# Mixer of a hybrid encoder: inverse norm roots by one GpSimd power, a bias negated on ScalarE, S5 steps earlier in the order

## The chip, the core and the metric

The kernel runs on one core of one Trainium2 chip. The metric is the device time of one execution in microseconds (us); the median of 3 runs of the kernel before is 2024.78 us (2024.78 to 2025.44). The core's engines each take their instructions from a queue of their own, strictly in order: TensorE (PE, matmuls and transposes), VectorE (DVE), ScalarE (ACT), GpSimd (POOL), and SyncE (SP, which issues the DMAs). They meet through semaphores only.

## What is computed

A trunk of two layers on x of 512 positions by 1024 features, all in float32. Each layer is a feed-forward block, a mixer with four head groups, and a second feed-forward block:

```python
for layer in range(DEPTH):                     # DEPTH = 2
    x = x + 0.5 * swiglu(rms_norm(x, ffn1_norm[layer]), ffn1_w_in[layer], ffn1_w_out[layer])
    x = x + hybrid_mixer(rms_norm(x, mix_norm[layer]), w_in[layer], ...)
    x = x + 0.5 * swiglu(rms_norm(x, ffn2_norm[layer]), ffn2_w_in[layer], ffn2_w_out[layer])

def hybrid_mixer(h, w_in, ...):
    aq, ak, av, bu, cq, ck, cv, dq, dk, dv = jnp.split(h @ w_in, splits, axis=-1)
    o_a, lse_a = banded_attention(rms_norm(heads(aq), ...), rms_norm(heads(ak), ...), heads(av), ...)
    y_b = s5_bidirectional(bu, lam_re, lam_im, ...)          # a complex diagonal recurrence, both ways
    y_b = g * jax.nn.sigmoid(g @ w_glu)                      # g = gelu(y_b)
    o_c = dilated_attention(rms_norm(heads(cq), ...), rms_norm(heads(ck), ...), heads(cv), ...)
    o_d = neighborhood_attention(rms_norm(heads(dq), ...), rms_norm(heads(dk), ...), heads(dv), rel_bias)
    return concatenate([o_a, y_b, o_c, o_d]) @ w_out
```

The queries and keys of groups A, C and D (aq, ak, cq, ck, dq, dk) are each scaled by the inverse root of their mean square: six norms in a mixer, twelve in the kernel. Five of the six have four heads (16 numbers to a partition), ak has two (8 numbers). Group D adds a learned relative bias and a mask to its scores.

## The kernel before, in words

**Products.** A float32 product is made of three matmuls, mm3 (L106 to L109): each operand is split into a high part, rounded to a type that the matmul takes, and the low remainder. weights() (L116 to L134) loads a block of weights (wr), rounds it on ScalarE (wh, L125) and subtracts on VectorE (wl, L126); in the mixer the subtraction is given to GpSimd instead (pooled=True).

**The mixer's pieces.** project() runs a projection of 512 positions as steps of matmuls into ppr. qk() (L549 to L606) takes a q or k projection: ScalarE copies it (L565) and squares it, VectorE sums the squares (L570), adds epsilon (L573, the tile ss), takes the inverse root (rn) and multiplies (four instructions at L579). flip() then transposes the result on TensorE (ptp, L589) and splits it in high (o, by ScalarE) and low (L603, by VectorE). s5() runs the recurrence: matmuls er and ei (per, pei), four VectorE products with the rotation (L810 to L813, out of PSUM), two GpSimd sums (zr, zi, L814 and L815), four scans on VectorE (sr, si, L823 and L825), the rotation back (zr, zi at L832 to L837, partly on GpSimd as rot), and matmuls pyp (L847 to L849). Attention heads: scores psc, the sum with the bias and its maximum p, mn (L680), exponentials on ScalarE, a scaling of p on GpSimd (L694), transposes (L713), copies pT (L715, L716), products pot (L718, L719), and the head's result m, split by L736 and L737 into mt. The merges mA to mD multiply mt by w_out (pop).

**The inverse root.** rsqrt() (L136 to L145) is eleven VectorE instructions: a shift and a subtraction on the bits as integers for a first guess (L140, L141), then three rounds of three (L143 to L145).

**What sets the order.** ORDER (L34 to L39) is a string of 116 tokens, written by hand: dq, dk, dv, cq and so on are a projection's steps (the fifth of a q or k is its flip), s5 the recurrence's steps, Ds and Dt (Cs, Ct, As, At) the two halves of a head, mB a merge step. The program is written out in this order; on each engine a scheduler places the instructions, and from then on each queue is fixed. Nothing is reordered at run time. Tile names carry a number in what follows (rn669 is one tile); tiles of before and of after have different numbers.

Of the kernel before, what the change touches and what calls it, by code (L numbers as in the profile page):

```python
# [32 lines left out]
BIG = 1e30  # L33
HOOK = 300  # L34
ORDER = """
dq dq dq dk dk dq dq dk s5 dk dv cq dk s5 Ds dv dv ck cq ck Ds cq dv Ds dv Ds Ds s5 cq s5 Dt ck s5 Dt s5 Dt ck
cq s5 Ds cv Dt aq cv s5 aq Ds Dt Dt Ds ck Cs cv Dt s5 cv aq ak aq Cs s5 ak Dt Cs aq Cs Ct ak mD ak Cs Ct Cs Cs
Ct ak Cs Ct s5 mD Ct mD As Ct As Ct Ct As mD As As At As As mB At As At At At mC mC mB mB mC At At mC At mC mC
mC mB mC mA mA  # L39
"""  # L40
T2 = 15
# [29 lines left out]
def hybrid_encoder(ctx: ExitStack, tc: tile.TileContext, t: dict):  # L71
# [61 lines left out]

        return at  # L134

    def rsqrt(y, v, shape):  # L136
        w = sml([P, 16], "rq")
        w = w[:, :shape[0]] if len(shape) == 1 else w.rearrange("p (a b) -> p a b", a=shape[0])[:, :, :shape[1]]
        yi = y.bitcast(I32)
        ts(yi, v.bitcast(I32), 1, None, op0=ALU.logical_shift_right)  # L140
        ts(yi, yi, -1.0, float(0x5F3759DF), op0=ALU.mult, op1=ALU.add)  # L141
        for _ in range(3):
            tt(w, y, y, op=ALU.mult)  # L143
            stt(w, w, -0.5, v, op0=ALU.mult, op1=ALU.mult)
            stt(y, w, 1.5, y, op0=ALU.add, op1=ALU.mult)  # L145

    ident = pool.tile([P, P], F32, name="ident")
    make_identity(nc, ident)
    ones2 = pool.tile([P, 2], F32, name="ones2")
    nc.vector.memset(ones2, 1.0)  # L150
    mhalf = pool.tile([P, 4], F32, name="mhalf")
    nc.vector.memset(mhalf, -0.5)
    ebase = pool.tile([P, G], F32, name="ebase")
    nc.vector.memset(ebase, E32)
# [11 lines left out]

    qkg = pool.tile([P, DEPTH, 6], F32, name="qkg")
    sink = pool.tile([P, DEPTH, 4], F32, name="sink")
    dmask = pool.tile([P, 7, 16], F32, name="dmask")
    for tl, nme in ((qkg, "qkg"), (sink, "sink"), (dmask, "dmask")):  # L170
        nc.gpsimd.dma_start(tl, t[nme])
    for i in (0, 2, 4):
        ts(qkg[:, :, i], qkg[:, :, i], -1.0, None, op0=ALU.mult)
# [314 lines left out]
    def mixer(l, T, next_norm):  # L488
# [63 lines left out]
        def qk(blk0, nh, perm, gi, res, extra=None):  # L552
# [4 lines left out]
            def norm():  # L557
                pts = st["pts"]
                if extra is not None:
                    extra(pts)  # L560
                ss = sml([P, 4, 4], "ss")
                for j in range(2):
                    q = t2(name="q")
                    qv = q.rearrange("p (b w) -> p b w", b=2)[:, :, :w]
                    nc.scalar.copy(qv, pts[j].rearrange("p (b w) -> p b w", b=2)[:, :, :w])  # L565
                    raw.append(qv)
                    sq = t2(name="sq")
                    sv = sq.rearrange("p (b w) -> p b w", b=2)[:, :, :w]
                    act(sv, qv, AF.Square)
                    nc.vector.tensor_reduce(ss[:, 2 * j:2 * j + 2, :nh], sv.rearrange("p b (h d) -> p b h d", d=64),  # L570
                                            axis=AX.X, op=ALU.add)
                sn = ss[:, :, :nh]
                tt(sn, sn, bc(ec, 2, nh), op=ALU.add)  # L573
                rn = sml([P, 4, 4], "rn")
                rsqrt(rn[:, :, :nh], sn, [4, nh])
                for j in range(2):
                    for b in range(2):
                        a = raw[j][:, b].rearrange("p (h d) -> p h d", d=64)
                        tt(a, a, bc(rn[:, 2 * j + b, :nh], 2, 64), op=ALU.mult)  # L579
# [81 lines left out]
        def attention(res, qk, vs, band, biases, perm, is_a):  # L661
# [35 lines left out]
            def second(i, part):  # L697
# [36 lines left out]
                if i % 2 == 1:  # L734
                    mt = k4([P, 2, S], F32R, name="mt")
                    nc.scalar.copy(mt[:, 0], m)  # L736
                    gtt(mt[:, 1], m, f32(mt[:, 0]), op=ALU.subtract)  # L737
                    res[i // 2].append(mt)

            return first, second  # L740
# [38 lines left out]

        def d_bias(i):  # L780
            b = bias_tile(t["rbx"][l, i], 896, True)
            for c0, m0, nk in ((0, 0, 2), (256, 2, 3), (640, 5, 2)):
                bv = b[:, c0:c0 + nk * P].rearrange("p (k u w) -> p k u w", u=8, w=16)
                tt(bv, bc(dmask[:, m0:m0 + nk], 2, 8), bv, op=ALU.subtract)
            return lambda q: b[:, 0:256] if q == 0 else (b[:, 640:896] if q == 3 else b[:, 256:640])

        def c_bias(i):
# [162 lines left out]
def _tables():  # L950
# [8 lines left out]
    mult = (dist <= 64) * 1 + ((dist % 4 == 0) & (dist <= 256)) * 1 + (dist % 16 == 0) * 1  # L959
    for i in range(4):  # L960
        ctab[i] = np.where(mult > 0, slopes[4 + i] * dist - np.log(np.maximum(mult, 1)), BIG)
    dmask = np.zeros((P, 7, 16), np.float32)
    ri = np.zeros((P, 896), np.int64)
    ci = np.zeros((P, 896), np.int64)
    r, c = np.arange(P) // 16, np.arange(P) % 16
    for qb, k0, k1, col, m0 in ((0, 0, 2, 0, 0), (1, 0, 3, 256, 2), (3, 2, 4, 640, 5)):
        qc = 16 * qb + c
        ws = np.clip(qc - 8, 0, 48)
        for kb in range(k0, k1):
            for u in range(8):  # L970
                for w in range(16):
                    kc = 16 * kb + w
                    j = col + (kb - k0) * P + u * 16 + w
                    dmask[:, m0 + kb - k0, w] = np.where((kc >= ws) & (kc < ws + 16), 0.0, BIG)
                    ri[:, j] = u - r + 7
                    ci[:, j] = np.clip(kc - qc + 15, 0, 30)
    return atab, ctab, dmask, ri, ci


def _layout(i):  # L980
# [56 lines left out]
        for c in range(16):  # L1037
            sd[:, 64 * (g % 2) + c, 3 * (g // 6) + g % 6 // 2, c] = dsk[:, g, c]
    a["s5d"] = sd
    a["atab"], a["ctab"], a["dmask"], ri, ci = _tables()  # L1040
    a["rbx"] = ac(np.asarray(i["na_rel_bias"])[:, :, ri, ci])
    return a


# [14 lines left out]
```

## Time and profile before

| | before |
|---|---|
| median of 3 runs | 2024.78 us |
| the profiled execution, its own time | 2025.69 us |
| its span in the trace | 2023.9 us |
| TensorE busy | 1969.1 us, 97% of the span |
| VectorE, ScalarE, GpSimd busy | 1240.6, 804.4, 368.4 us (61%, 40%, 18%) |

The profiled execution stands 0.9 us above the median; 1.8 us of it lie outside the span. The two mixers take up about 404 to 665 us and 1408 to 1669 us of the span and show the same pattern of waits; the times quoted from here on are those of the first. A line's number is that of the kernel before. "Idle before" is how long an engine stood still ahead of an instruction, and the name behind the arrow is whose semaphore came last. PEclk is the granted clock of TensorE as a share of its full speed: 1.00 is 2.4 GHz, 0.50 is 1.2 GHz.

### The profile page before, as it was taken

To read this page: it belongs to the slowest core of one execution; us is meant where nothing else is said; L and a number is where in the kernel's file an instruction comes from. 1 tells how busy PE (TensorE), PEld (TensorE's weight loads), DVE (VectorE), ACT (ScalarE), POOL (GpSimd) and SP (SyncE) were. 2 spreads that over 40 slices of the span, in tenths; PEclk is the share of its full clock that TensorE was granted. 3 is DMA by queue.
4 is the path that set the end of the run, shared out by engine and by line. 5 is a ranking of instruction groups with operands and counts; after the bars stand their busy time and mean duration, and the time that the engine had idled before them with its cause. 6 is when DMAs were issued, how large, how long until landed. Compare 5 with 4: busy or idle time off the path is not lost.

```text
span 2023.9 us, 26161 instructions
## 1 busy us (share of the span) xinstructions
PE 1969.1 (97%) x9768; PEld 1648.9 (81%) x9768; DVE 1240.6 (61%) x2327; ACT 804.4 (40%) x1523; POOL 368.4 (18%) x349
## 2 busy tenths in 40 slices
PE   8999999998999999999999999999989989999999
PEld 6788878897977788888888888888978778888887
DVE  6865547657887545444577655465687875444454
ACT  4333323444676323233442333334547653232332
POOL 4010100254445000000120101002544540000000
PEclk9999999998999999999999999999989999999999
DMA  5232343331312332323233332423313122333233
GB/s 176 82 104 88 104 83 106 97 114 51 97 55 72 97 101 91 97 89 109 84 116 88 102 93 93 102 88 103 119 39 99 50 66 94 99 96 103 81 107 104
DMA packets 74447, 189.24 MB, mean 93 GB/s; under 512 B 16960, under 2 KB 22848, under 8 KB 74320
## 3 DMA queue, kind: packets, MB, share of 16 engines
q1 hardware_dynamic: 74224, 187.51, 30.7%
q8 instruction: 76, 1.25, 0.3%
q14 instruction: 51, 0.42, 0.1%
q0 software_dynamic: 96, 0.07, 0.0%
HBM read 182.86 MB, written 4.69 MB: 93 GB/s over the span
## 4 chain that ended last, share of the span: by engine, by line
PE 83%; DVE 10%; ACT 4%; issue 2%; POOL 1%; DMA 0%; SPq 0%; DVEq 0%; ACTq 0%; POOLq 0%
PE pop L109 9%; PE pop L108 9%; PE pop L107 9%; PE pup L107 7%; PE pgp L107 7%; PE pgp L108 7%; PE pgp L109 7%; PE pup L109 7%; PE pup L108 7%; PE ppr L107 1%; PE ppr L108 1%; PE ppr L109 1%; DVE wl L126 1%; PE pfp L448 1%; DVE hl L186 1%
## 5 line engine op out<-in xcount | busy, mean ns | idle before, releaser
L125 ACT CAST wh<-wr 128x512 fp32r<-128x512 f32 (+2 forms) x718 | 405.9, 570 | 962.8 <-PE pgp L109 314.0
L126 DVE TENSOR_TENSOR wl<-wr,wh 128x512 fp32r<-128x512 f32 (+2 forms) x618 | 409.4, 665 | 380.0 <-ACT wh L125 378.3
L107 PE MATMUL pgp<-hh,wl 128*128 128x512 f32 x704 | 275.5, 391 | 7.6 <-DVE wl L126 7.6
L107 PE MATMUL pup<-hh,wl 128*128 128x512 f32 x704 | 276.3, 392 | 3.2 <-DVE wl L126 3.2
L107 PE MATMUL pop<-a,wl 128*128 128x512 f32 x704 | 277.0, 395 | 1.4 <-DVE wl L126 1.4
L108 PE MATMUL pgp<-hl,wh 128*128 128x512 f32 x704 | 275.5, 391 | 2.4 <-DVE hl L186 2.4
L109 PE MATMUL pop<-a,wh 128*128 128x512 f32 x704 | 276.3, 392 | 0.0
L108 PE MATMUL pop<-a,wh 128*128 128x512 f32 x704 | 274.5, 390 | 0.6 <-DVE a L257 0.6
L108 PE MATMUL pup<-hl,wh 128*128 128x512 f32 x704 | 275.0, 391 | 0.0
L109 PE MATMUL pup<-hh,wh 128*128 128x512 f32 x704 | 275.0, 391 | 0.0
L109 PE MATMUL pgp<-hh,wh 128*128 128x512 f32 x704 | 274.7, 390 | 0.0
L196 POOL TENSOR_TENSOR t<-t,sq 128x512 f32<-128x512 f32 x42 | 60.0, 1430 | 664.9 <-ACT sq L195 663.6
L107 PEld LDWEIGHTS pgp<-hh,wl 128*128 128x128 f32 x704 | 132.6, 188 | 35.7 <-DVE wl L126 8.0
L126 POOL TENSOR_TENSOR wl<-wr,wh 128x512 fp32r<-128x512 f32 (+1 forms) x100 | 131.2, 1317 | 161.7 <-ACT wh L125 125.4
L107 PEld LDWEIGHTS pup<-hh,wl 128*128 128x128 f32 x704 | 132.5, 188 | 33.6 <-DVE wl L126 5.6
L108 PEld LDWEIGHTS pgp<-hl,wh 128*128 128x128 f32 x704 | 132.6, 188 | 32.9 <-DVE hl L186 5.5
L109 PEld LDWEIGHTS pop<-a,wh 128*128 128x128 f32 x704 | 132.2, 188 | 30.6
L108 PEld LDWEIGHTS pop<-a,wh 128*128 128x128 f32 x704 | 132.2, 188 | 30.2 <-DVE a L257 1.0
L107 PEld LDWEIGHTS pop<-a,wl 128*128 128x128 f32 x704 | 132.3, 188 | 28.9 <-DVE wl L126 2.1
L109 PEld LDWEIGHTS pup<-hh,wh 128*128 128x128 f32 x704 | 132.4, 188 | 27.6
L109 PEld LDWEIGHTS pgp<-hh,wh 128*128 128x128 f32 x704 | 132.4, 188 | 27.6
L108 PEld LDWEIGHTS pup<-hl,wh 128*128 128x128 f32 x704 | 132.5, 188 | 27.4
(263 smaller groups left out, 3071.3 us busy)
## 6 DMA issues: line engine op xcount, KB each, us to landing
wr<-in_f_w SPq DMA_DIRECT2D x176, 512.0 KB, 3.4
wr<-in_f_w SPq DMA_DIRECT2D x64, 384.0 KB, 3.1
wr<-in_f_w SPq DMA_DIRECT2D x64, 320.0 KB, 2.9
wr<-in_wm SPq DMA_DIRECT2D x36, 512.0 KB, 3.5
bias<-in_ctab SPq DMA_DIRECT2D x8, 448.0 KB, 3.4
bias<-in_rbx SPq DMA_DIRECT2D x8, 448.0 KB, 3.8
wr<-in_woC SPq DMA_DIRECT2D x8, 384.0 KB, 3.1
x<-in_xt SPq DMA_DIRECT2D x8, 256.0 KB, 6.4
```

Source lines behind the costliest of these rows:

```text
L107: nc.tensor.matmul(out, ll, rh, start=start, stop=False)
L108: nc.tensor.matmul(out, lh, rl, start=False, stop=False)
L109: nc.tensor.matmul(out, lh, rh, start=False, stop=stop)
L125: nc.scalar.copy(hi[:, :w], r)
L126: (nc.gpsimd if pooled else nc.vector).tensor_tensor(lo[:, :w], r, f32(hi[:, :w]), op=ALU.subtract)
L186: stt(hl, x[c], gcol, f32(hh), op0=ALU.mult, op1=ALU.subtract)
L196: gtt(acc, acc, sq, op=ALU.add)
L448: nc.tensor.matmul(pt[r0:r0 + 64, c0 + 16:c0 + 144], bm[q][:, g].rearrange("p a c -> p (a c)"), v[q][:, g].rearrange("p j c -> p (j c)"), ...
```

## The change

Four edits, all in the mixer:

- rsqrt() goes. The norm's root is one GpSimd power, rn = ss to the power of -0.5 (gtt at L567 of after), over 128x16 for four heads and 128x8 for ak's two; the tile of exponents mhalf is widened to 16.
- The low half of mt (L737) moves from GpSimd to VectorE.
- D's bias: before, VectorE subtracts it from a mask in three instructions for a head (L784); now the mask is put into the bias on the host and ScalarE negates it by one copy with a scale of -1 over 128x896.
- ORDER: S5's steps come sooner. The first stands after the third dq instead of after the third dk.

```diff
-dq dq dq dk dk dq dq dk s5 dk dv cq dk s5 Ds dv dv ck cq ck Ds cq dv Ds dv Ds Ds s5 cq s5 Dt ck s5 Dt s5 Dt ck
-cq s5 Ds cv Dt aq cv s5 aq Ds Dt Dt Ds ck Cs cv Dt s5 cv aq ak aq Cs s5 ak Dt Cs aq Cs Ct ak mD ak Cs Ct Cs Cs
-Ct ak Cs Ct s5 mD Ct mD As Ct As Ct Ct As mD As As At As As mB At As At At At mC mC mB mB mC At At mC At mC mC
+dq dq dq s5 dq s5 dk dk dk dq dk s5 dv s5 dk dv cq s5 Ds dv s5 dv ck cq ck Ds s5 cq dv Ds s5 Ds Ds cq Dt ck Dt
+Dt ck cq Ds cv Dt aq cv aq Ds s5 Dt Dt Ds ck Cs cv Dt cv aq ak aq s5 Cs ak Dt Cs aq Cs s5 Ct ak mD ak Cs Ct Cs
+Cs Ct ak Cs Ct mD Ct mD As Ct As Ct Ct As mD As As At As As mB At As At At At mC mC mB mB mC At At mC At mC mC
...
-                rsqrt(rn[:, :, :nh], sn, [4, nh])
+                if nh == 4:
+                    sn, rv, half = (a.rearrange("p b h -> p (b h)") for a in (ss, rn, mhalf.rearrange("p (b h) -> p b h", b=4)))
+                else:
+                    rv, half = rn[:, :, :nh], mhalf.rearrange("p (b h) -> p b h", b=4)[:, :, :nh]
+                gtt(rv, sn, half, op=ALU.pow)
...
-                    gtt(mt[:, 1], m, f32(mt[:, 0]), op=ALU.subtract)
+                    tt(mt[:, 1], m, f32(mt[:, 0]), op=ALU.subtract)
...
-            for c0, m0, nk in ((0, 0, 2), (256, 2, 3), (640, 5, 2)):
-                bv = b[:, c0:c0 + nk * P].rearrange("p (k u w) -> p k u w", u=8, w=16)
-                tt(bv, bc(dmask[:, m0:m0 + nk], 2, 8), bv, op=ALU.subtract)
+            act(b[:, :896], b[:, :896], AF.Copy, scale=-1.0)
```

On the engines this makes VectorE's queue 2130 instructions long instead of 2274, GpSimd's 343 instead of 344, ScalarE's 1435 instead of 1429; outside the two mixers no queue changes its order.

**VectorE, cq's norm, before.** The place is the end of cq's norm in the first mixer (ss773 to rn778), among S5's rotation back (zi682) and the copies of D's first head (pT):

```order
L140 TENSOR_SCALAR rn778_4158<-ss773_4146 128x16
L141 TENSOR_SCALAR rn778_4158<-rn778_4158 128x16
L143 TENSOR_TENSOR rq779_4159<-rn778_4158 128x16
L144 SCALAR_TENSOR_TENSOR rq779_4159<-rq779_4159,ss773_4146 128x16
L145 SCALAR_TENSOR_TENSOR rn778_4158<-rq779_4159,rn778_4158 128x16
...
L837 TENSOR_TENSOR zi682_3640<-zi682_3640,rot791_4233 128x512
L145 SCALAR_TENSOR_TENSOR rn778_4158<-rq779_4159,rn778_4158 128x16
L716 TENSOR_TENSOR pT795_4253<-ptp794_4249,pT795_4253 128x384
L579 TENSOR_TENSOR q774_4147<-q774_4147,rn778_4158 128x256 x2
```

S5's zi stands behind ten of the norm's eleven instructions; the norm's products with q follow.

**VectorE, dk's norm, after.** S5's scans now come during D's projections. This is the queue from dq's products (q667, the second half) to dk's (q691, q693, with rn695):

```order
L571 TENSOR_TENSOR q667_3528<-q667_3528,rn669_3534 128x256 x2
...
L561 TENSOR_TENSOR ss690_3704<-ss690_3704,ec636_3348 128x16
L813 SCALAR_TENSOR_TENSOR si697_3723<-k480_2623,zi659_3471 64x1023
L815 SCALAR_TENSOR_TENSOR si697_3723<-k480_2623,zi659_3471 64x1023
...
L813 SCALAR_TENSOR_TENSOR sr696_3722<-k480_2623,zr658_3470 64x1023
L815 SCALAR_TENSOR_TENSOR sr696_3722<-k480_2623,zr658_3470 64x1023
L825 TENSOR_TENSOR zi659_3471<-si697_3723,k478_2621 128x512 x2
...
L632 TENSOR_TENSOR vb711_3803<-a710_3801,R635_3346 128x8x4x16
L571 TENSOR_TENSOR q691_3705<-q691_3705,rn695_3716 128x256 x2
L571 TENSOR_TENSOR q693_3710<-q693_3710,rn695_3716 128x256 x2
```

Between dk's sum of squares (ss690) and its products now stand four scans, two products of S5 and three low halves of dq (left out here, o at L595). Before, dk's products followed its eleven small instructions directly, with no scan between.

**GpSimd, the same stretch, before**, in the mixer's D projections:

```order
L126 TENSOR_TENSOR wl680_3612<-wr676_3605,wh679_3611 128x512
L126 TENSOR_TENSOR wl696_3723<-wr694_3720,wh695_3722 128x512
L815 TENSOR_TENSOR zi682_3640<-zi682_3640,rot686_3660 128x512
L814 TENSOR_TENSOR zr681_3639<-zr681_3639,rot685_3659 128x512
L126 TENSOR_TENSOR wl698_3727<-wr694_3720,wh697_3726 128x512
L126 TENSOR_TENSOR wl702_3746<-wr700_3743,wh701_3745 128x512
```

**and after**, with the two powers of dq (rn669) and dk (rn695):

```order
L804 TENSOR_TENSOR zr658_3470<-zr658_3470,rot662_3490 128x512
L567 TENSOR_TENSOR rn669_3534<-ss664_3522,mhalf_70 128x16
L805 TENSOR_TENSOR zi659_3471<-zi659_3471,rot673_3559 128x512
L804 TENSOR_TENSOR zr658_3470<-zr658_3470,rot672_3558 128x512
L126 TENSOR_TENSOR wl683_3629<-wr681_3626,wh682_3628 128x512
L126 TENSOR_TENSOR wl685_3633<-wr681_3626,wh684_3632 128x512
...
L567 TENSOR_TENSOR rn695_3716<-ss690_3704,mhalf_70 128x16
L126 TENSOR_TENSOR wl714_3808<-wr712_3805,wh713_3807 128x512
L823 TENSOR_TENSOR rot719_3841<-si697_3723,k479_2622 128x512
L126 TENSOR_TENSOR wl716_3812<-wr712_3805,wh715_3811 128x512
L826 TENSOR_TENSOR rot720_3842<-sr696_3722,k479_2622 128x512
L126 TENSOR_TENSOR wl730_3869<-wr728_3866,wh729_3868 128x512
```

S5's sums come ahead of the weights of dv and cq, a power stands between them, and four weights and two rotations follow the second power.

**TensorE, S5's result, before and after.** Before, one matmul of pyp818 that reads zi682 stands among cq's projection and D's heads, and the rest right behind it:

```order
L109 MATMUL ppr830_4422<-wh788_4204,hh580_3121 128x256
L718 MATMUL pot780_4181<-pT795_4253,v757_4063 128x384
L849 MATMUL pyp818_4362<-zi682_3640,s279_1564 128x64
L847 MATMUL pyp818_4362<-u2640_3359,tm414_2319 128x64
L848 MATMUL pyp818_4362<-zr681_3639,s278_1563 128x64
```

After, dk's transposes (ptp704, ptp707) and, 100 rows behind them, S5's pyp751, all 24 matmuls in one piece:

```order
L109 MATMUL ppr718_3816<-wh701_3736,hh580_3119 128x256
L581 MATMUL ptp704_3759<-ident_63,q691_3705 128x2x4x16
L581 MATMUL ptp707_3774<-ident_63,q691_3705 128x2x4x16
L107 MATMUL ppt733_3876<-hh589_3153,wl716_3812 128x512
...
L109 MATMUL ppr743_3923<-wh731_3872,hh580_3119 128x256
L837 MATMUL pyp751_4016<-u2640_3357,tm414_2317 128x64
L838 MATMUL pyp751_4016<-zr658_3470,s278_1561 128x64
L839 MATMUL pyp751_4016<-zi659_3471,s279_1562 128x64
```

S5's result is asked for earlier in the mixer, right behind D's v and the first scores, and dk's transposes come 92 rows behind dq's.

## Rows read from the trace of the kernel before

**Rows 1.** The page's part 1: each engine's busy us, share, instructions.
```profile
PE 1969.1 (97%) x9768; PEld 1648.9 (81%) x9768; DVE 1240.6 (61%) x2327; ACT 804.4 (40%) x1523; POOL 368.4 (18%) x349
```
**Rows 2.** Window: length, busy us (count) of PE, PEld, DVE, ACT, POOL, PEclk, DMA.
```profile
475.00:500.00 25.00, 17.51 (x108) 16.58 (x108) 20.99 (x39) 6.80 (x16) 13.76 (x12) 0.77 0.14 43
```
**Rows 3.** TensorE's waits over the whole span: us in total, times, longest.
```profile
PE pyp L849 <- DVE zi L837: 11.3, 2, 5.7
PE pot L719 <- DVE pT L716: 5.8, 8, 1.2
...
PE pop L107 <- ACT mt L885: 3.2, 2, 1.6
...
PE pop L108 <- POOL mt L737: 2.3, 4, 0.9
```
**Rows 4.** Timeline of TensorE, the longest wait: start, us, instruction, [idle before <-releaser].
```profile
491.90 0.69 PE L849 MATMUL pyp<-zi,s 128*128 128x64 f32 x2 [5.67 <-DVE zi L837]
```
**Rows 5.** Windows of 4 us at 488 and at 588 (PEclk third from right).
```profile
488.00:492.00 4.00, 0.10 (x1) 0.10 (x1) 3.79 (x10) 0.00 (x0) 2.17 (x2) 0.55 0.43 131
492.00:496.00 4.00, 4.00 (x19) 4.00 (x20) 2.07 (x6) 0.00 (x0) 0.00 (x0) 0.50 0.00 0
...
504.00:508.00 4.00, 4.00 (x30) 4.00 (x29) 2.58 (x6) 2.92 (x6) 0.60 (x1) 0.82 0.00 0
...
588.00:592.00 4.00, 2.82 (x9) 1.85 (x10) 4.00 (x8) 3.03 (x7) 4.00 (x4) 0.85 0.01 2
592.00:596.00 4.00, 4.00 (x14) 3.16 (x14) 2.85 (x4) 0.36 (x3) 0.50 (x1) 0.72 0.37 102
```
**Rows 6.** Timeline of VectorE ahead of that wait, cq's norm and zi.
```profile
485.31 1.23 DVE L141 TENSOR_SCALAR rn<-rn 128x16 int32<-128x16 int32 x1
...
490.24 0.17 DVE L143 TENSOR_TENSOR rq<-rn 128x16 f32<-128x16 f32 x1
...
491.16 0.68 DVE L837 TENSOR_TENSOR zi<-zi,rot 128x512 f32<-128x512 f32 x1
```
**Rows 7.** Timeline of GpSimd beside it.
```profile
486.48 1.25 POOL L126 TENSOR_TENSOR wl<-wr,wh 128x512 fp32r<-128x512 f32 x1
```
**Rows 8.** Groups by line: busy us, mean ns; a GpSimd subtraction and ScalarE's rounding.
```profile
L737 POOL TENSOR_TENSOR mt<-m,mt 128x512 fp32r<-128x512 f32 x12 | 16.4, 1364 | 33.0 <-ACT mt L736 33.0
...
L125 ACT CAST wh<-wr 128x512 fp32r<-128x512 f32 (+2 forms) x718 | 405.9, 570 | 962.8 <-PE pgp L109 314.0
```
**Rows 9.** Timeline: a GpSimd power of 128x16 (S5's tables), VectorE during it.
```profile
40.59 2.91 POOL L302 TENSOR_TENSOR sm<-ebase,sm 128x16 f32<-128x16 f32 x1 [11.44 <-DMA sm<-in_s5lam]
...
41.91 0.68 DVE L126 TENSOR_TENSOR wl<-wr,wh 128x512 fp32r<-128x512 f32 x1
```
**Rows 10.** Timeline of TensorE: the mixer's first matmuls, two kinds in line.
```profile
403.18 0.95 PE L203 MATMUL pst<-ones,t 128*128 128x2 f32 x8
...
432.64 0.28 PE L109 MATMUL ppr<-wh,hh 128*128 128x256 f32 x1
432.76 0.40 PE L107 MATMUL ppt<-hh,wl 128*128 128x512 f32 x1
433.00 0.40 PE L108 MATMUL ppt<-hl,wh 128*128 128x512 f32 x1
```
**Rows 11.** Timeline of VectorE: q's products with and without GpSimd beside them, two scans.
```profile
439.34 2.51 DVE L579 TENSOR_TENSOR q<-q,rn 128x256 f32<-128x256 f32 x4
...
492.32 1.42 DVE L579 TENSOR_TENSOR q<-q,rn 128x256 f32<-128x256 f32 x4
...
469.70 2.83 DVE L823 TENSOR_TENSOR_SCAN si<-k,zi 64x1023 f32<-64x1023 f32 x1
472.55 2.29 DVE L825 TENSOR_TENSOR_SCAN si<-k,zi 64x1023 f32<-64x1023 f32 x1
```
**Rows 12.** Timeline of GpSimd beside the products and the scan of Rows 11.
```profile
439.78 1.45 POOL L126 TENSOR_TENSOR wl<-wr,wh 128x512 fp32r<-128x512 f32 x1 [2.04 <-ACT wh L125]
...
467.40 3.00 POOL L126 TENSOR_TENSOR wl<-wr,wh 128x512 fp32r<-128x512 f32 x1 [3.01 <-ACT wh L125]
```

More of the change, by code (lines that the diff above doesn't have):

```diff
@@ L134, in weights @@
         return at
[L136 to L145, printed above, removed]
     ident = pool.tile([P, P], F32, name="ident")
@@ L150, in hybrid_encoder @@
     nc.vector.memset(ones2, 1.0)
-    mhalf = pool.tile([P, 4], F32, name="mhalf")
+    mhalf = pool.tile([P, 16], F32, name="mhalf")
     nc.vector.memset(mhalf, -0.5)
@@ L168, in hybrid_encoder @@
     sink = pool.tile([P, DEPTH, 4], F32, name="sink")
-    dmask = pool.tile([P, 7, 16], F32, name="dmask")
-    for tl, nme in ((qkg, "qkg"), (sink, "sink"), (dmask, "dmask")):
+    for tl, nme in ((qkg, "qkg"), (sink, "sink")):
         nc.gpsimd.dma_start(tl, t[nme])
@@ L961, in _tables @@
         ctab[i] = np.where(mult > 0, slopes[4 + i] * dist - np.log(np.maximum(mult, 1)), BIG)
-    dmask = np.zeros((P, 7, 16), np.float32)
+    seen = np.zeros((P, 896), bool)
     ri = np.zeros((P, 896), np.int64)
@@ L965, in _tables @@
     r, c = np.arange(P) // 16, np.arange(P) % 16
-    for qb, k0, k1, col, m0 in ((0, 0, 2, 0, 0), (1, 0, 3, 256, 2), (3, 2, 4, 640, 5)):
+    for qb, k0, k1, col in ((0, 0, 2, 0), (1, 0, 3, 256), (3, 2, 4, 640)):
         qc = 16 * qb + c
@@ L973, in _tables @@
                     j = col + (kb - k0) * P + u * 16 + w
-                    dmask[:, m0 + kb - k0, w] = np.where((kc >= ws) & (kc < ws + 16), 0.0, BIG)
+                    seen[:, j] = (kc >= ws) & (kc < ws + 16)
                     ri[:, j] = u - r + 7
                     ci[:, j] = np.clip(kc - qc + 15, 0, 30)
-    return atab, ctab, dmask, ri, ci
+    return atab, ctab, seen, ri, ci
 def _layout(i):
@@ L1039, in _layout @@
     a["s5d"] = sd
-    a["atab"], a["ctab"], a["dmask"], ri, ci = _tables()
-    a["rbx"] = ac(np.asarray(i["na_rel_bias"])[:, :, ri, ci])
+    a["atab"], a["ctab"], seen, ri, ci = _tables()
+    a["rbx"] = ac(np.where(seen, np.asarray(i["na_rel_bias"])[:, :, ri, ci], np.float32(-BIG)))
     return a
```

## The prediction

> **What bounds the kernel now.** I read the engines' busy time first. TensorE works 97% of the span [rows 1]: whatever the change does, it can only be felt where TensorE stands still or runs at its lower clock. The windows come next. In the feed-forward blocks there is nothing to win, and no queue is changed there; the worst stretch of a mixer is 475 to 500 us, with 17.51 of 25 us busy and a mean granted clock of 0.77 [rows 2]. Then TensorE's waits, which name the culprits over both mixers [rows 3]: S5's result waits 11.3 us in two waits (5.65 a mixer) for VectorE's zi; the merge of S5's GLU waits 3.2 us in two (1.6 a mixer); the low half of mt on GpSimd costs 2.3 us (1.15 a mixer); the copies pT cost 5.8 us in eight waits, 0.73 each. The timeline places the long one at 491.90 [rows 4].
>
> The windows of 4 us show what follows a stop [rows 5]. The clock is at 0.55 during the long wait, stays at 0.50, which is 1.2 GHz, from 492 to 504 and is back to 2.4 GHz in the window after that. TensorE is busy there, so it loses 3 x 4 x 0.50 + 4 x 0.18 = 6.7 us. Behind the wait of 1.6 us the clock gives 0.85 and 0.72 in two windows, 4 x 0.15 + 4 x 0.28 = 1.7 us.
>
> Why is zi late? VectorE's and GpSimd's timelines side by side tell it. zi, 0.68 us of work, stands in VectorE's queue behind cq's norm. The norm's small instructions take 0.17 us when nothing is beside them, but 1.23 us while GpSimd runs its subtractions of 1.25 us [rows 6, 7]: two-input work of both engines takes turns. That is the behaviour on which the sum depends. Four products of q take 2.51 us with one GpSimd subtraction beside them and 1.42 without; a scan takes 2.83 us beside one and 2.29 without [rows 11, 12]. One GpSimd subtraction so costs VectorE 1.1 us in the one case and 0.55 in the other.
>
> **The change, part by part.** All sums are for one mixer; the second repeats it.
>
> *Gone.* The norms' small instructions (eleven each, 132 in all) leave VectorE, so none stands ahead of S5's zi any more. In after, VectorE finishes zi some 15 instructions behind dk's products, within 10 us of them, while TensorE has 100 matmuls, 12 of 0.23 and the rest about 0.12 us [rows 10], 13 us, between dk's transposes and pyp751: whatever holds dk's products, S5's result is there first. So the wait of 5.65 and its 6.7 us at the low clock go. S5's GLU is ready sooner too, so 1.6 + 1.7 go. The low half of mt takes 0.68 us on VectorE, as other subtractions there [rows 9], instead of 1.36 [rows 8], and its 1.15 us of waits go. Sum: 5.65 + 6.7 + 1.6 + 1.7 + 1.15 = 16.8 us.
>
> *Costs nothing on TensorE's path.* Twelve more subtractions on VectorE are 8.2 us in all, 24 bias subtractions go from it; VectorE has 39% of the span free [rows 1]. ScalarE's eight negations have no row; the rounding of 512 columns takes 0.57 us [rows 8], so 896 columns are about 1.0 us by width. They stand between copies of a head, well ahead of the scores that read them; if one is waited for, it costs at most its 1 us, as the pT waits do. It is among the small waits below.
>
> *GpSimd's queue.* It loses 12 x 1.36 = 16.4 us [rows 8] and gets twelve powers. A power of 128x16 takes 2.91 us [rows 9], so twelve take at most 35. GpSimd is busy 18% [rows 1], so its total is no matter; its order is. A power waits for VectorE's sum of squares, and behind it stand S5's sums and the weights' low halves that TensorE needs next.
>
> *dq's norm.* TensorE first. From the mixer's first matmul at 403.18 [rows 10], 0.8 us of statistics, 192 matmuls of 256 columns at 0.12 us [rows 10] and 32 small ones of S5 at about the same (0.8 + 26.9 = 27.7) and the start's wait bring it to dq's transposes at about 432.4. The norm: S5's first sums end on GpSimd at 427.4, the sum of squares is ready at 428.2, the power ends at 431.15. Then VectorE's four products take turns with zi, zr, wl683 and wl685, which are then ready on GpSimd: 4 x (1.25 + 0.36) = 6.4, done at 437.6, transposes at 438.1 instead of 433.2: 4.9 us lost. Without turns, only wl683 (third in GpSimd's queue, at 431.15 + 3 x 1.28 = 435.0) holds TensorE: 1.8. Ends 1.8 and 4.9; I take 4.9, since the nearest row, the same four products, shows turns [rows 11].
>
> *dk's norm.* TensorE needs 36 x 0.23 + 48 x 0.12 = 14.1 us [rows 10] from there, so it is at dk's transposes at 452.2. VectorE can't multiply before it has done what stands ahead: o 0.68, the addition 0.17, two scans 4.6, two o 1.4, two scans 4.6, two products 1.4, o 0.68, vb 0.68 and the first product 0.36 [rows 6, 11], 14.4 us from 438.5, so 452.9, and 454.0 for the fourth. Before, no scan stood there. So 1.7 us late without any turns. Six GpSimd subtractions and rotations lie in the same stretch; each a full turn of 1.25 us makes 7.5 more, so 9.3 late. At the measured price, 0.55 for the four scans and 1.1 for two short ones, 4.4 more, so 6.1. I take 6.1 and keep 1.7 and 9.3. The low clock is bounded by 1.7 us (the short wait's) and 6.7 (the long one's). When the clock falls after dq's wait, TensorE comes to dk's transposes later, and the same lateness is filled by slow matmuls; so the likely case has one of the two, 6.1, and not their sum.
>
> *Small waits.* Three are new: the second projection's first matmul waits for VectorE at the mixer's start; the last pT and scores of D's heads have no projection between them; cq's products meet GpSimd's subtractions. At 0.7 us each [rows 3], 2.1.
>
> Added: 2.1 + 4.9 + 6.1 = 13.1. Removed: 16.8. Gain 3.7 a mixer, 7.4 in all. The profiled execution of 2025.69 becomes 2018.3; the median stands 0.9 lower, so **2017 us**.
>
> A page bears on this. The Trainium skill, SBUF — State Buffer, section "Who interferes with whom", says that a VectorE instruction with two SBUF inputs and a GpSimd instruction that reads SBUF exclude each other for the whole instruction. For the subtractions the rows agree. By that rule a power, which reads SBUF, would shut such work out for its 2.91 us. The rows speak against it: VectorE's subtraction in the middle of S5's power takes 0.68 us as ever [rows 9]; no run here shows a norm's power. What it would change is the fourth rival.
>
> **The rivals.**
>
> *1. dk's products wait in full (slower).* GpSimd has its next subtraction ready at each turn, so dk's products come 9.3 us after TensorE, and the clock falls behind that wait as it did behind 5.65 us: 2.1 + 4.9 + 9.3 + 6.7 = 23.0, a loss of 6.2 a mixer, 12.4 in all: 2037. It decides where dk's products come later than 16.8 - 2.1 - 4.9 - 6.7 = 3.1 us after TensorE and the low clock is as long as before. For it: six GpSimd instructions do stand in that stretch. Against: two of them need the scans' results, and beside scans the rows show 0.55, not 1.25.
>
> *2. No turns at the norms (faster still).* 2.1 + 1.8 + 1.7 + 1.7 = 7.3, a gain of 9.5 a mixer, 19 in all: 2006. For it: weights that come late leave GpSimd idle. Against: zi and zr are ready by then.
>
> *3. The wait only moves.* The S5 wait goes and the norms take 16.8 us back: 2025. Any lateness of 3 us with the full low clock does so.
>
> *4. The power excludes VectorE.* The power for dk meets the scans: 2.9 us more a mixer, 5.8 in all, 2023. The row shows otherwise.
>
> **How the numbers follow.** Chances: forecast 0.36, rival 1 0.27, rival 2 0.18, rival 3 0.14, rival 4 0.05. Repeated measurements can tell about 0.2%, 4 us, from no change. Faster by more: 0.26 of the forecast's, all of rival 2, 0.02 of rival 3: 0.46. Within: 0.10 + 0.06 (rival 1 in part) + 0.10 + 0.03: 0.29. Slower: the rest of rival 1 and 0.02 each of rivals 3 and 4: 0.25. The range goes from a little below rival 2, 2003, to rival 1, 2037; it leaves out the case that nothing is added at all (2025.7 - 33.6, less 0.9, 1991) and that the second half of the mixer waits as well, where the attention's last C and A pieces have no merge between them. The forecast's own range is 2010 to 2024.
>
> **What would show it.** In the profile of after: pyp should be absent from TensorE's waits, or under 1 us. ptp should appear in them with VectorE's q as releaser, twice a mixer near 433 and 453, at about 5 us or less. The clock's windows near 492 to 504 should be 1.00, those behind 453 tell rival 1 from the forecast. GpSimd's power should show about 2.9 us; VectorE's scans near 440 to 450, 2.3 without turns, 2.8 as I price them, 3.5 and more for rival 1; a scan of 5 us beside a power speaks for rival 4. Wrong would be a wait for pyp that remains, or a lower clock in a stretch with no wait of VectorE's.

## The result and the profile after

The changed kernel takes **2044.34 us** (median of 4 runs, 2038.09 to 2044.77) against 2024.78: a ratio of 1.0088, 95% interval 1.0075 to 1.0100. It is slower by 0.9%, where 2017 was forecast and 2037 was the range's end. Its runs fall in two groups, one at 2038.1 and three at 2044.3 to 2044.8; what may stand between them comes below. The profiled execution is of the upper group: 2044.77 us, a span of 2042.8.

The page's part 1 of the kernel after (busy us, share, count) shows what the change was to bring. VectorE has lost 34 us of work and GpSimd has got 26; TensorE stands still 9.3 us longer and is busy 9.6 us longer, which makes the span's growth of 18.9:

```profile
PE 1978.7 (97%) x9768; PEld 1649.7 (81%) x9768; DVE 1206.6 (59%) x2183; ACT 809.4 (40%) x1531; POOL 394.6 (19%) x348
```

At the same count of matmuls, busy time grows where the clock is low, and also where TensorE stops more often: a matmul of 512 columns that is followed at once gives way to the next after 0.23 us, and ahead of a stop the whole 0.39 us count for which it stands in the trace. Some 2 us of the 9.6 are the low clock (the section on the prediction adds this up). All of the loss lies in the mixers. Measured from the first matmul of a mixer's statistics to that of the next block's, the first grew from 264.5 to 276.6 us, the second from 264.2 to 270.9; the two feed-forward blocks between them took 739.4 and 739.5.

TensorE's waits over the whole span of after, in us in total, times, longest (they answer to [rows 3]):

```profile
PE ptp L581 <- DVE q L571: 16.0, 10, 6.7
PE pop L107 <- ACT mt L728: 9.0, 6, 2.2
...
PE psc L669 <- DVE mn L672: 4.1, 8, 1.0
PE pot L710 <- ACT pT L707: 3.2, 8, 1.0
PE ptp L705 <- POOL p L686: 2.8, 2, 1.4
PE ppr L107 <- DVE us L499: 2.5, 2, 1.3
...
PE per L798 <- DMA u<-ud: 1.1, 1, 1.1
```

The 11.3 us for S5's zi are gone, as are the wait for the GLU and that for mt's low half. In their place stand transposes that wait for VectorE's products with the norm (16.0), and waits in the second half that were not there or smaller (pop for mt's high half 9.0, of which one of 2.2 in each mixer is new). TensorE's timeline has them in place, in the first mixer:

```profile
411.71 0.38 PE L107 MATMUL ppr<-wh,hl 128*128 128x256 f32 x1 [1.27 <-DVE us L499]
...
423.26 1.97 PE L798 MATMUL per<-u,s 128*128 128x64 f32 x16 [1.11 <-DMA u<-ud]
...
467.06 0.66 PE L581 MATMUL ptp<-ident,q 128*128 128x128 f32 x2 [6.68 <-DVE q L571]
...
571.15 1.30 PE L705 MATMUL ptp<-ident,p 128*128 128x128 f32 x8 [1.42 <-POOL p L686]
...
656.46 0.94 PE L107 MATMUL pop<-mt,wl 128*128 128x512 f32 x3 [2.23 <-ACT mt L728]
```

and, in the second mixer, the transposes of dq (twice) and dk:

```profile
1453.86 0.41 PE L581 MATMUL ptp<-ident,q 128*128 128x128 f32 x2 [0.93 <-DVE q L571]
1455.17 0.44 PE L581 MATMUL ptp<-ident,q 128*128 128x128 f32 x2 [0.90 <-DVE q L571]
...
1476.28 0.66 PE L581 MATMUL ptp<-ident,q 128*128 128x128 f32 x2 [5.29 <-DVE q L571]
```

Windows of 4 us of after, for the granted clock (third number from the right), at three times in the first mixer:

```profile
424.00:428.00 4.00, 4.00 (x29) 4.00 (x28) 1.30 (x3) 0.00 (x0) 0.00 (x0) 0.73 0.28 115
428.00:432.00 4.00, 4.00 (x20) 4.00 (x20) 2.47 (x4) 1.22 (x2) 2.51 (x2) 0.50 0.01 4
...
440.00:444.00 4.00, 4.00 (x25) 4.00 (x24) 4.00 (x5) 1.11 (x2) 4.00 (x4) 0.63 0.00 0
...
468.00:472.00 4.00, 4.00 (x17) 3.30 (x16) 3.67 (x8) 1.64 (x3) 2.12 (x5) 0.72 0.58 229
...
656.00:660.00 4.00, 3.54 (x11) 2.81 (x12) 2.62 (x4) 1.68 (x4) 0.00 (x0) 0.75 0.37 133
```

From 424 to 444 us TensorE is busy all the time, in the three middle windows at 0.50, which is 1.2 GHz: 4 x (0.27 + 3 x 0.50 + 0.37) = 8.6 us lost. The second mixer has no such stretch. That is most of what separates the first mixer's growth (12.1) from the second's (6.7). By its size it may also be what separates the two groups of runs, 6.3 us apart; no run of after's lower group was profiled.

Around dk's norm VectorE and GpSimd run like this in the first mixer of after; VectorE first:

```profile
440.03 4.83 DVE L571 TENSOR_TENSOR q<-q,rn 128x256 f32<-128x256 f32 x4
...
448.82 2.27 DVE L813 TENSOR_TENSOR_SCAN si<-k,zi 64x1023 f32<-64x1023 f32 x1
451.13 2.29 DVE L815 TENSOR_TENSOR_SCAN si<-k,zi 64x1023 f32<-64x1023 f32 x1
...
457.32 3.22 DVE L815 TENSOR_TENSOR_SCAN sr<-k,zr 64x1023 f32<-64x1023 f32 x1
460.57 3.27 DVE L825 TENSOR_TENSOR zi<-si,k 128x512 f32<-128x512 f32 x2
...
465.44 3.56 DVE L571 TENSOR_TENSOR q<-q,rn 128x256 f32<-128x256 f32 x4
```

and GpSimd:

```profile
435.20 2.92 POOL L567 TENSOR_TENSOR rn<-ss,mhalf 128x16 f32<-128x16 f32 x1 [3.93 <-DVE ss L561]
...
448.99 4.83 POOL L567 TENSOR_TENSOR rn<-ss,mhalf 128x16 f32<-128x16 f32 x1 [0.61 <-DVE ss L561]
...
455.03 3.36 POOL L823 TENSOR_TENSOR rot<-si,k 128x512 f32<-128x512 f32 x1
458.36 3.25 POOL L126 TENSOR_TENSOR wl<-wr,wh 128x512 fp32r<-128x512 f32 x1
```

dq's four products take 4.83 us (1.42 with nothing beside them [rows 11]). dk's power is ready at 453.82, but its products begin at 465.44, behind the four scans and S5's first products: the queue that the prediction walked.

### The profile page after: what moved, and what is told of

Its sections match the earlier page's. It is cut to its first block, busy times and chain, and to the rows that moved or that the text cites. A ratio compares the mean times of both kernels' runs of the same rounds, so it can differ in the third digit from the quotient of the medians.

```text
span 2042.8 us, 26034 instructions
## 1 busy us (share of the span) xinstructions
PE 1978.7 (97%) x9768; PEld 1649.7 (81%) x9768; DVE 1206.6 (59%) x2183; ACT 809.4 (40%) x1531; POOL 394.6 (19%) x348
## 3 DMA queue, kind: packets, MB, share of 16 engines
q8 instruction: 76, 1.25, 0.3%
## 4 chain that ended last, share of the span: by engine, by line
PE 84%; DVE 8%; ACT 3%; issue 2%; POOL 1%; DMA 1%; SPq 0%; DVEq 0%; ACTq 0%; POOLq 0%
PE pop L107 9%; PE pop L109 9%; PE pop L108 9%; PE pup L107 7%; PE pgp L107 7%; PE pgp L108 7%; PE pgp L109 7%; PE pup L108 7%; PE pup L109 7%; PE ppr L108 2%; PE ppr L107 2%; PE ppr L109 2%; DVE wl L126 1%; PE ptp L705 1%; PE pfp L436 1%
```

## The experiments

Fifteen kernels ran on the chip beside before and after. The table gives each median with that of the kernel before in the same session, and the two mixers' lengths in the profiled execution, measured as above, in one execution each. "Power" is the GpSimd power, "bias" the negation on ScalarE, "low half" mt's low half on VectorE.

| kernel | what it is | median us | before | mixer 1 | mixer 2 |
|---|---|---|---|---|---|
| before | | 2024.78 | | 264.5 | 264.2 |
| after | all four edits | 2044.34 | 2024.78 | 276.6 | 270.9 |
| e_old_order | power, bias, low half | 2019.95 | 2024.95 | 261.1 | 261.6 |
| e_new_order | new ORDER alone | 2058.11 | 2024.95 | 281.3 | 278.7 |
| e_pow_only | power alone | 2009.74 | 2025.27 | 256.4 | 257.2 |
| e_old_mtpool | power, bias | 2013.06 | 2025.27 | 259.3 | 257.3 |
| e_mtlo_pool | power, bias, new ORDER | 2033.72 | 2025.27 | 266.7 | 269.1 |
| e_new_pow | power, new ORDER | 2035.57 | 2025.66 | 270.0 | 267.5 |
| e_d_only | after, S5's tokens at their old places | 2015.34 | 2025.66 | 258.8 | 258.4 |
| e_er_early | e_d_only, S5's steps 1 and 2 early | 2028.36 | 2025.51 | 271.7 | 262.9 |
| e_scan_early | e_d_only, S5's steps 1 to 8 early | 2033.96 | 2025.51 | 267.0 | 269.6 |
| e_scans_late | after, S5's steps 3 and 4 later | 2047.10 | 2024.95 | 279.2 | 274.1 |
| e_u_late | after, S5's steps 1 and 2 one token later | 2038.43 | 2024.95 | 270.5 | 271.3 |
| e_glu_late | after, S5's last step later | 2036.91 | 2025.27 | 274.3 | 270.5 |
| e_pow_glu1 | power, S5's last step 2 places sooner | **2003.80** | 2025.66 | 253.3 | 253.4 |
| e_pow_glu3 | power, S5's last step 5 places sooner | 2011.50 | 2025.66 | 255.0 | 257.3 |
| e_best2 | power, D's new order, last step 2 sooner | 2012.64 | 2025.51 | 257.9 | 257.7 |

### The order against the other edits

e_old_order is after with the ORDER of before, e_new_order before with that of after:

```diff
-dq dq dq s5 dq s5 dk dk dk dq dk s5 dv s5 dk dv cq s5 Ds dv s5 dv ck cq ck Ds s5 cq dv Ds s5 Ds Ds cq Dt ck Dt
+dq dq dq dk dk dq dq dk s5 dk dv cq dk s5 Ds dv dv ck cq ck Ds cq dv Ds dv Ds Ds s5 cq s5 Dt ck s5 Dt s5 Dt ck
...
```

> The changed kernel with the ORDER of before: the power, the bias on ScalarE and mt's low half on VectorE remain, S5's steps stand where they stood. Theory O (the order costs, the other edits are harmless): 2005 to 2025 us, dk's products wait under 1.5 us, and the second half of a mixer is as long as before within 2 us. Rival P (the power on GpSimd costs, wherever S5 stands): 2035 us or more, with TensorE's transposes waiting 5 us or more for q in both mixers.

> The kernel before with the ORDER of after, nothing else: the inverse root stays on VectorE. Theory O: 2035 us or more, the transposes of dk wait 4 us or more behind the scans, and the second half of each mixer is some 7 us longer than before. Rival P: 2025 us or less, since no power is there.

2019.95 (ratio 0.9975, interval 0.9966 to 0.9984) and 2058.11 (1.0166, 1.0151 to 1.0181): the order costs 24 us beside the other edits and 33 without them. The rival that the power costs wherever S5 stands is out. In e_new_order, where the norms are VectorE's eleven instructions still, the waits of the transposes are longer than in after:

```profile
PE ptp L589 <- DVE q L579: 25.1, 5, 9.6
PE psc L677 <- DVE mn L680: 9.1, 9, 2.5
```

So the power helps in both orders. Two points of theory O missed, both on the second half of a mixer, from the last projection matmul on. Before takes 110.9 us there. With the old order e_old_order takes 113.3 and 115.5, so some of the other edits do cost there; and the new ORDER alone (e_new_order) takes 113.5 and 112.2, 1.3 to 2.6 us more and not some 7. The order alone is not what makes that half 9.4 us longer in after.

### The edits one by one

e_pow_only is before with the power, e_new_pow that with the new ORDER; e_old_mtpool adds the bias to e_pow_only; e_mtlo_pool is after with one line turned back:

```diff
-                    tt(mt[:, 1], m, f32(mt[:, 0]), op=ALU.subtract)
+                    gtt(mt[:, 1], m, f32(mt[:, 0]), op=ALU.subtract)
```

> The kernel before with the GpSimd power alone. If the gain of the edits is the power's (VectorE rid of eleven small instructions a norm), it is within 3 us of the kernel with power and bias, 2009 to 2017; if the bias on ScalarE has a part in it, it lies 5 us or more above that one.

> The kernel before with the power and the bias on ScalarE, and nothing else of the change (ORDER and mt's low half of before). Theory M with theory O: 2009 to 2015 us, the fastest so far, since the edits on the norm gain and neither the order nor the low half costs. Rival (mt's low half on VectorE helps): slower than 2020.

> The changed kernel with mt's low half back on GpSimd. Theory M (the second half of a mixer grew in part because the list scheduler, seeing a quick low half, puts the last merge's first matmul right behind the last head's products: a wait of 2.2 us for mt's high half and a low clock behind it): the wait of 2.2 us at the mixer's end goes, 15 merge matmuls stand between, 3 to 5 us less a mixer, 2034 to 2038. Rival (the low half itself is quicker on VectorE by 0.7 us and that counts): 2044 to 2050.

> The kernel before with the power and the new ORDER, without the other two edits. If the order's cost and the other edits' costs add up, it is the kernel of power alone (2009.7) plus some 20 us, 2027 to 2034, and the transposes of dk wait 3 us or more behind the scans in both mixers. Rival (the order only costs together with mt's low half or the bias on ScalarE): 2018 us or less.

The power alone gives 2009.74, a ratio of 0.9921 (0.9906 to 0.9936): 15.5 us won. TensorE's waits in e_pow_only say where most of it lies: the wait for zi, 11.3 us in before [rows 3], is 2.1 with no step of S5 moved.

```profile
PE pop L107 <- ACT mt L889: 7.8, 2, 3.9
PE psc L681 <- DVE mn L684: 5.2, 6, 2.7
PE pop L107 <- ACT mt L740: 3.6, 2, 1.8
...
PE pyp L853 <- DVE zi L841: 2.1, 2, 1.1
```

The new ORDER added to it costs 25.8 us (e_new_pow, a little above the range expected), with the transposes' waits of 15.9 us, the longest 5.3. The bias is 3.3 us slower in the old order and 1.9 faster in the new one: small, and of no settled sign. The low half on VectorE costs 6.9 us in the old order and 10.6 in the new, by medians. The 10.6 are not all its own: after's profile has the 8.6 us of low clock at 424 to 444 us and e_mtlo_pool's has not. Between the second mixers, where neither has it, there are 1.8 us (269.1 and 270.9), and after's one run of the lower group lies 4.4 above e_mtlo_pool's median. So the cost is clear in the old order, 6.9 us, and smaller than 10.6 in the new. That was the surprise, since the instruction itself takes half the time there.

In the old order the waits for mt's high half grow with it, in e_old_mtpool (low half on GpSimd) and in e_old_order (on VectorE):

```profile
PE pop L107 <- ACT mt L728: 3.6, 2, 1.8
PE pop L107 <- ACT mt L728: 8.5, 4, 2.6
```

TensorE's queue in the new order shows a like pair. The end of the first mixer in after, and in e_mtlo_pool (the last products of the last head, pot, and the first merge matmul that needs its result, with the tile mt 5889; "..." stands for 15 rows of pop with other tiles):

```
after:        L710 MATMUL pot_5840<-pT_5881,v_5127 128x384
              L711 MATMUL pot_5840<-pT_5881,v_5127 128x384
              L107 MATMUL pop_5972<-mt_5889,wl_5927 128x512

e_mtlo_pool:  L710 MATMUL pot_5840<-pT_5881,v_5127 128x384
              L711 MATMUL pot_5840<-pT_5881,v_5127 128x384
              ...
              L107 MATMUL pop_5972<-mt_5889,wl_5927 128x512
```

With the low half on VectorE the merge stands right behind the head's products, and 15 merge matmuls with other tiles ahead of them; that the list scheduler does so because it sees a quick low half is a reading of the order, not shown. In after, TensorE then waits 2.23 us for the high half, which ScalarE makes in both kernels, and the clock falls to 0.75 (the row at 656.46 and the window above). With it on GpSimd the 15 matmuls between, 3.4 us at 0.23, cover that way. In e_mtlo_pool the waits for mt are four of at most 1.8 us:

```profile
PE pop L107 <- ACT mt L728: 6.1, 4, 1.8
```

Here the order of the queue changed, not only the engine. No kernel moved the low half at a fixed order, so how much of its cost is this gap at the end and how much lies elsewhere in the queue is open.

### Which of S5's early steps

The change of ORDER also sorts D's own tokens anew, so e_d_only puts S5's eleven tokens back and keeps the rest; e_er_early and e_scan_early move two and eight of them forward again.

```diff
 e_d_only
-dq dq dq s5 dq s5 dk dk dk dq dk s5 dv s5 dk dv cq s5 Ds dv s5 dv ...
+dq dq dq dq dk dk dk dq s5 dk dv dk dv s5 cq Ds dv dv ck cq ck Ds cq dv Ds Ds Ds s5 cq s5 Dt ...
```

> The changed kernel with S5's eleven tokens at the places of before and the other tokens in the order of after. The new order costs 24 us beside the same other edits. Theory E (S5's steps being early cost them): 2018 to 2026. Rival D (the order of D's own projections and flips, which also changed, costs them): 2036 us or more.

> The changed kernel with S5's first two tokens (er, ei, the rotation in) at the new early places and its nine others at the places of before. Theory R (S5's early products and GpSimd's sums around dq's power already cost a good part): 2022 us or more, with waits of dq's transposes. Theory N (the scans and what follows cost, the first two steps do not): 2012 to 2019, like the kernel with all of S5 at the old places (2015).

> The changed kernel with S5's first eight tokens at the new places and the last three (its output, its GLU) at the places of before. Theory N: nearly all of the early steps' cost is in these eight, 2034 to 2044, with the wait of 5 us and more for dk's products. Rival (the last three, through the merges, cost as much): 2026 to 2031.

D's order is not the cost: 2015.34, 29 us faster than after and 4.6 faster than e_old_order. By medians, steps 1 and 2 early cost 13 us, steps 3 to 8 another 5.6, the last three about 10. These differences are not clean: the profiles of e_er_early and after have a low clock behind er that e_scan_early's has not. The second mixers, where er waits in none of them, give 4.5 us a mixer for steps 1 and 2 (258.4 to 262.9), 6.8 for steps 3 to 8 (to 269.6) and 1.3 for the last three (to 270.9), each from one execution. So the scans and what follows them cost most, steps 1 and 2 not nothing, and the last three little: theory N is right about the scans and wrong about the first two steps. The profile of e_er_early tells that the first cost is in part not the one that I looked for. Its second mixer is 4.5 us longer than e_d_only's, its first 12.9, and there the wait for u's DMA and the low clock behind it are back, with S5's scans at their old places. TensorE's timeline:

```profile
423.36 1.97 PE L798 MATMUL per<-u,s 128*128 128x64 f32 x16 [1.32 <-DMA u<-ud]
```

and windows of 4 us behind it (the clock third from the right):

```profile
424.00:428.00 4.00, 4.00 (x29) 4.00 (x28) 1.29 (x2) 0.00 (x0) 0.00 (x0) 0.72 0.17 71
428.00:432.00 4.00, 4.00 (x20) 4.00 (x21) 2.48 (x4) 1.22 (x2) 2.51 (x2) 0.50 0.01 4
432.00:436.00 4.00, 4.00 (x21) 4.00 (x20) 1.37 (x3) 0.00 (x0) 0.55 (x1) 0.50 0.00 0
```

In e_scan_early, whose er found u landed (no wait for it), these windows are at 1.00, and the 5 us for dk's products stand in both mixers (15.6 us in 12 waits for q, the longest 5.1).

e_u_late was to take the wait for u away, by one token:

```diff
-dq dq dq s5 dq s5 dk dk dk ...
+dq dq dq dq s5 dk s5 dk dk ...
```

> The changed kernel with S5's first step one token later (behind the fourth dq). Theory U (in the first mixer er waits 1.1 us for the DMA of u, and this wait brings the low clock from 424 to 443 us): no wait for u, granted clock 1.00 in the windows of 424 to 444, first mixer 5 to 8 us shorter, second mixer within 2 us, 2035 to 2039. Rival C (the low clock comes with the 32 small matmuls of S5 or by chance): the clock is low there still, 2042 to 2046.

It did not: er still waited 0.94 us for the DMA. Yet the clock stayed at 1.00 from 424 to 444 us and the first mixer took 270.5 us instead of 276.6; of its four runs three took 2038.0 to 2038.6 and one 2045.16. So this kernel has the same two groups as after, and its median tells mainly how many runs fell in each; that the profiled run, of the lower group, has no low clock there fits the reading that the low clock makes the groups. Over all profiles with a wait of er, the low clock stands behind waits of 1.11, 1.32 and 1.60 us, and not behind 0.66, 0.72, 0.94, 1.04 and 1.36. The wait alone does not decide; what does is open.

e_scans_late asked whether dk's products are late because the scans stand ahead of them:

```diff
-dq dq dq s5 dq s5 dk dk dk dq dk s5 dv s5 dk dv cq s5 ...
+dq dq dq s5 dq s5 dk dk dk dq dk dv dk s5 dv s5 cq s5 ...
```

> The changed kernel with two tokens moved: S5's third and fourth step (the scans) stand behind dk's flip instead of ahead of it. Theory S (dk's products wait because the four scans stand ahead of them in VectorE's queue): the waits of 6.68 and 5.29 us for q fall under 2 us each and the time falls by 8 to 14 us, to 2030 to 2036. Rival G (GpSimd's queue, with a power that takes 4.8 us and turns with VectorE, holds dk's products): a wait of 4 us or more remains and the time stays above 2038.

The first half of theory S held: the waits for q fell to 0.9 us at most. Its time did not follow: 2047.10. What stood behind the products stands behind the scans now, in TensorE's timeline of this kernel:

```profile
463.95 0.53 PE L670 MATMUL psc<-kl,o 128*128 128x256 f32 x2 [3.69 <-DVE kl L595]
468.33 0.58 PE L108 MATMUL ppr<-wl,hh 128*128 128x256 f32 x1 [3.56 <-POOL wl L126]
```

VectorE's low half of dk (kl) waits for the four scans, and GpSimd's weights take turns with them: 7.25 us in place of 6.68. Four scans of 2.3 us are 9.1 us of VectorE at a place where TensorE needs it every few microseconds; in before they ran from 464 to 474 us, where TensorE's waits beside them came to 1.8 us.

### S5's last step

e_glu_late moves S5's last token of after back; e_pow_glu1 and e_pow_glu3 move it forward in e_pow_only, whose longest wait in the mixers is that for the GLU's result (3.9 us):

```diff
 e_glu_late
-Cs s5 Ct ak mD ak Cs Ct Cs Cs Ct ak Cs Ct mD Ct mD
+Cs Ct ak mD ak Cs Ct Cs Cs Ct ak Cs Ct s5 mD Ct mD
 e_pow_glu1, e_pow_glu3
-Cs Cs Ct ak Cs Ct s5 mD Ct mD
+Cs Cs Ct ak s5 Cs Ct mD Ct mD
+s5 Cs Cs Ct ak Cs Ct mD Ct mD
```

> The changed kernel with S5's last step (its GLU) moved back behind the fourth-last C half, as in the kernel before. Theory L (an early GLU lets the merges run early, so that the last C and A heads have no merge matmuls between them): 3 to 8 us less, 2036 to 2041, and fewer waits between 561 and 602 us. Rival (the order of the GLU is no matter, the growth of the second half is the low half of mt alone): 2042 to 2046.

> The kernel of power alone with S5's last token two places sooner (ahead of the last C head's first half), to relieve the wait of 3.9 us for S5's GLU result at 580 us. If only this wait is moved out, 3 to 8 us less than 2009.7 (2002 to 2007). If the merges it frees run early and leave the last heads without filler, as in the changed kernel: 2009 or more.

> The same with the last S5 token five places sooner, close to its place in the changed kernel. By the theory of early merges the GLU wait is gone and other waits of psc, pot and ptp in the second half grow by as much or more: 2008 to 2016. If an early GLU is simply good: 2003 or less.

e_glu_late's median is 7.4 us below that of after, but with runs from 2034.68 to 2043.27 it has two groups too; its profiled mixers are 2.3 and 0.4 us shorter, and the wait for the GLU is back (6.4 us in two). In the first mixer the low clock behind er is shorter too, 6.8 us instead of 17.1, which alone is worth 5 us. So an early last step costs after next to nothing by the second mixer, and theory L is not shown. Two places sooner in the old order gains 5.9 us on the power alone: **2003.80 us, 0.9891 of before (0.9876 to 0.9906), the fastest kernel of the study.** Five places sooner it takes 2011.50, as expected: the wait for the GLU is gone there too, but the waits for mt's high half rise from 3.6 to 5.8 us and new ones of 3.8 us stand for ScalarE's pT.

```diff
 e_best2 (on e_pow_only: D's tokens in the new order, S5's at the old places but the last)
+dq dq dq dq dk dk dk dq s5 dk dv dk dv s5 cq ... Cs Cs Ct ak s5 Cs Ct mD Ct mD ...
```

> The power alone, the new order of D's tokens, S5 at the places of before but its last token two places sooner. If the gain of D's order (4.6 us beside all edits) adds to the fastest kernel so far (2003.8): 1997 to 2002. If they overlap: 2003 to 2006.

2012.64, above both ranges: D's order, worth 4.6 us beside all edits, costs 8.8 here. Gains of an order don't add.

## Why the prediction was wrong

It forecast a gain of 7.4 us and the span grew by 18.9. The forecast's terms fall into idle time of TensorE and time lost to the low clock. The trace of after gives both, and a third part for which the sum had no term: the same 1542 matmuls of a mixer take longer on record at the full clock. All three are changes from before to after, in us a mixer:

| | forecast | mixer 1 | mixer 2 |
|---|---|---|---|
| TensorE idle | +4.7 | +4.0 | +4.9 |
| lost to the low clock while busy | -8.4 | +5.0 | -2.8 |
| the same matmuls at full clock | none | +3.1 | +4.6 |
| sum | -3.7 | +12.1 | +6.7 |

The idle time came out as forecast, but by luck, since its parts did not. The third row goes with the number of stops, which the walk of single waits leaves out: TensorE stands still 25 times in a mixer of before, 41 and 43 times in those of after, and the last matmul ahead of a stop is not overlapped by the next (0.39 and not 0.23 us for 512 columns; the trace models a matmul's end). By the prediction's own steps, for one mixer:

- **S5's wait goes (5.65 + 6.7): right, but credited to the wrong edit.** pyp is in no wait of after, and the clock is at 1.00 at that place. The power alone brings the wait from 11.3 to 2.1 us over both mixers (e_pow_only). I had shown myself that zi stood behind the norm's instructions, and still took the early steps to be part of the cure. They had little left to cure, so nearly all their costs are net.
- **GLU (1.6 + 1.7) and mt's low half (1.15) go: the step that failed.** Those very waits are gone; the half behind them is not shorter. From the last projection matmul to the end of the mixer, before takes 110.9 us and after 120.3, in both mixers, where 4.45 less was forecast. TensorE's idle time there rose from 9.1 to 13.4 us and the time lost to the low clock from 3.3 to 4.9; of the other 3.5 us some 1.5 are eleven matmuls more that stand behind the cut, and TensorE stops 26 times there instead of 16. I read these edits by the waits that they take away and did not walk the queue behind them. The text named the place where new waits could come and left it out of the range; and I moved the low half to VectorE "at 0.68 instead of 1.36" without asking where the merges would then stand. It cost 6.9 us over both mixers in the old order (e_old_order against e_old_mtpool), where 2.3 less was forecast. The GLU's term is not wrong in kind: two places sooner on the power alone it brought 5.9 us, close to 2 x 3.3, and five places sooner it lost 1.8.
- **dq's norm, 4.9: too high.** The second mixer shows 0.93 + 0.90 = 1.8 us, though the four products took 5.78 there for the turns: TensorE takes them two by two, as they come. The sum also counts the loss from 433.2, though it has TensorE there at about 432.4, and does not say why. In the first mixer the low clock brought TensorE late enough to wait for none.
- **dk's norm, 6.1: right in its wait.** 6.68 and 5.29 us, and by the mechanism that was walked. The low clock behind it, for which the forecast had nothing beside the 6.1, cost 1.6 and 2.2 us.
- **Small waits, 2.1: mis-sized by one missing term.** The start's wait rose by 0.58 as counted. Missing was the DMA of u, which er now meets; the text has no term for it. It is 1.1 us, and in the first mixer of after 8.6 us of low clock follow.
- **The bias, counted as nothing: nearly so.** It cost 3.3 us in the old order and gained 1.9 in the new.

Rival 1 came nearest, at 2037: its sign was right, but not its terms. It had dk's products 9.3 us late, and they were 6.68 and 5.29, as in the forecast; it had the full low clock of 6.7 behind them, and that was 1.6 and 2.2; and it had neither the second half's growth, nor u, nor the cost of more stops. That its 2037 lies near 2044 is chance. Rival 3's idea, that the wait only moves, is what e_scans_late shows. On turns, the prediction takes as its example a row of a one-input instruction (L141, 1.23 us [rows 6]), so what it calls two-input work is held up with one input too, at least there.

Rival 4 drew on the Trainium skill, SBUF — State Buffer, section "Who interferes with whom", by which a VectorE instruction with two SBUF inputs and a GpSimd instruction that reads SBUF exclude each other for a whole instruction. The rows agree for the start of a power: the one at 448.99 came 0.17 us behind a scan and took 4.83 us, 1.9 more than alone, which is about the rest of that scan. They differ for its length: the next scan, at 451.13, ran its usual 2.29 us while the power went on to 453.82. The second mixer shows the same pair (4.91 us, and a scan of 2.28 beside its end). So in these rows a power waits for a scan, and the scan does not wait for the power.

## What to carry over

A wait that is read in a profile has often one cause in one queue; take that one away alone first, and time it, before any other edit gets the credit. Here one edit of four carried all the gain (15.5 us), and the three others, to the order and the engines around it, cost 35 together. Where a scheduler fills the queues, moving an instruction to a faster engine can come with another order of what covers it: read the consumer's queue, not only the instruction's time. And a sum of waits is not the whole of what stops cost: count the stops too. Before medians are subtracted, look in the profiles for a stretch that one kernel has and the other has not, such as the low clock behind u here.

## What the runs showed of the hardware

- Work of VectorE and GpSimd on SBUF takes turns also at full size: four products 4.83 and 5.78 us instead of 1.42, some scans 3.2 instead of 2.3, GpSimd's subtraction 3.25 instead of 1.25 beside scans. A GpSimd power of 128x16 takes 2.9 us alone and did not slow the scan that came next while it ran, in both mixers.
- The granted clock fell behind a wait as short as 1.1 us in some runs and stayed up behind 1.36 us in another, at the same place. Where it fell, TensorE stayed busy at 1.2 GHz for 17.1 us before it rose in two kernels (after, e_er_early) and for 6.8 us in a third (e_glu_late).
- A matmul of 512 columns stands 0.39 us in the trace and the next starts 0.23 us behind it; ahead of a stop the whole 0.39 counts. Sixteen to eighteen more stops a mixer went with 3.1 and 4.6 us more of full-clock busy time.
